# A second weight block loaded ahead of the query weights, and the last stage's order laid anew

## The chip, the cores and the metric

The kernel runs on one core of one Trainium2 chip. The metric is device time in microseconds (us) of one launch, smaller is better. A core has a tensor engine (PE) for matrix products, a vector engine (DVE, VectorE), a scalar engine (ACT, ScalarE), a third general engine (POOL, GpSimd) and a queue engine (SP) that issues DMA transfers. Each engine works through its own instructions in a fixed order and waits by semaphore for the others. PE writes its sums to eight banks of a small memory (PSUM), and ACT or DVE must read a bank out before it can be used again.

## The reference, cut to what matters

One layer of a hybrid decoder on a prompt of 1024 tokens and on 8 x 8 sample tokens that attend to a paged cache of 8192 positions each:

```
n = rmsnorm(h);  u = n @ w_in                       # one projection, split by columns
o_gla = gated linear attention(gq, gk, gv, gg, ga)  # 4 heads
cq = rmsnorm(mq);  q = cq @ mla_w_qup               # 8 heads
k, v = rmsnorm(mkv) @ mla_w_kvup ...
o_mla = attention(q, k, v)                          # causal, and over the cache
h = h + concat(o_gla, o_mla) @ w_o
h = h + conv_ffn(rmsnorm(h))                        # gate, up, conv of width 3, down
h = h + (p @ ple_w_proj) * sigmoid(rmsnorm(h) @ ple_w_gate)
```

The outputs are h for prompt and samples, and the new latents, states and convolution rows. All inputs are float32. Products are made from a high and a low half of each operand (`x = high + low`), as three products: high x high, high x low, low x high. So each weight that is loaded is cast on ACT to its high half and subtracted on DVE or POOL to give its low half before PE can use it.

## The kernel before

The work runs in stages: an opening (sample tokens, the first half of the prompt), a long middle in which the projections, gated linear attention and prompt attention are woven with a stream over the cache blocks, the output projection, the feed-forward part, its last products (by a scheme of seven products instead of eight, the last of them called product 4), and a last stage: the per-layer embedding with its gate.

In the opening and the middle the builder of the program lays each engine's order: it goes by the order of the program as priority and by the readiness that it expects. The opening runs in `prompt_half(0)`. `load_mix(c0)` loads a block of 128 columns of `w_in` (two transfers of 256 KB through the staging buffers `stage`, of which there are three), casts it on ACT and subtracts on POOL, into one of three weight buffers (`wtile`). `load_q` loads the query weights (four transfers of 192 KB, two weight buffers), `load_kv` the key-value weights (two transfers of 256 KB, into two buffers `xin` that the sample work uses too). `mix` runs over blocks: `load_mix`, then `proj` (24 products on PE into `ps_pj`), then `post`, which adds the sample tokens' 8 products (`ps_sm`). The plan is `PLAN = ([0], [], [1, 2, 3])`: block 0 first, none in the second place, then blocks 1, 2, 3, each ahead of the heads of one 128-token tile. The sample tokens' query goes through `sample_q`, `q_finish` (a chain of small DVE and ACT operations; `nwt` is one of them, lines 121 to 125), the transposes `pt_q` (line 439), `ps_qp` (line 443) and `pt_qr` (line 449), under a raised priority.

```
wq = load_q()
wkh, wkl = load_kv()
for i in range(4):
    cT = latents_T(i)
    yield from mix(PLAN[2][i:i + 1])
    yield from heads(i, *cT)
```

In the last stage the order is written out by hand: `LAST` is a string of 370 names of steps, each of which issues an instruction or a few, and every engine keeps the order in which its steps stand in the string. A name's letters are the step, its last digit the tile of 128 rows (t) or the weight chunk (k). Those that the text speaks of:

- `f0`..`f3`: the folds of product 4's four sums into h (DVE, line 2331); `sq` the squares for the norm (ACT, line 1485), `st` a store of the folded part (POOL), `rt` the root (POOL)
- `Y`, `Tb`, `Ta`: four small transposes each of a part of h (PE, line 2202) into one of three banks `pd`; `ry` (line 2553), `ra` copy a turned part out (ACT), `e`, `i`, `g`, `j` form sums of parts (DVE)
- `ac`/`al`, `ic`/`il` and so on: cast (ACT) and low half (DVE) of an operand; `wc`/`wl`, `cc`/`cl`, `zc`/`zl`, `vc`/`vl`, `nc`/`nl`, `xc`/`xl` the same for the weight chunks of the gate's seven products (W, T3, T1, T2, T4, "22"), `c`, `z`, `v`, `n` their sums (DVE)
- `P1t`, `P2t`, `P7t`, `P6t`, `P5t`, `P4t`, `P3t`: twelve products of one tile (PE, `ps_pg`); `P33` is made in two halves. `Jnt`: six products of the embedding (`ps_pj`). `sA`, `sB`, `sC`, `sJ0`, `sJ1`: products of the sample tokens
- `Cq`, `Cv`, `Cw`, `Cx` (gate sum, DVE), `Cs` (sigmoid, ACT), `Cm`, `Ca` (times the embedding, plus h, DVE), `Co` (store of the output); `sd1`, `sk1`, `sm1`, `sa1`: the end of the samples' second half (ACT, DVE, DVE, DVE with a store through POOL); `cv`/`cvc` the convolution's rows; capital `W C Z V X N JL` the loads on SP

Of the kernel before, what the change touches and what calls it, by code (L numbers as in the profile page):

```python
# [18 lines left out]
P = 128  # L19
# [19 lines left out]
LAST = (  # L39
# [14 lines left out]
VIAP = 20  # L54
GS0 = 1
NWB = 10
# [11 lines left out]
def step_kernel(ctx: ExitStack, tc: tile.TileContext, A):  # L68
# [191 lines left out]
    def wtile():  # L260
        return wp.tile([P, 2 * D], F32R, tag="w", name="w")

    def wpair(kc, n):

        w = wtile()
        return tuple(w[:, s * kc * n:(s + 1) * kc * n].rearrange("p (k c) -> p k c", c=n) for s in range(2))

    def load_q():
        return [wload(wp, A["mla_w_qup"][0][:, f * 384:(f + 1) * 384], 2, 384, "w", sbufs=3, out=wpair(2, 384))
                for f in range(2)]  # L270

    def load_kv():
        hl = [wk.tile([P, 1, D], F32R, tag="xin", name="wkv") for _ in range(2)]
        return [w[:, 0] for w in wload(wp, A["mla_w_kvup"][0], 1, D, "w", sbufs=3, out=hl)]

    def load_mix(c0, lo_eng=pool):

        w = wtile().rearrange("p (k s c) -> p k s c", k=8, s=2)
        hl = wload(wp, w_in[:, c0:c0 + P], 8, P, "w", sbufs=3, lo_eng=lo_eng, out=(w[:, :, 0], w[:, :, 1]))
        return hl + (w,)  # L280
# [255 lines left out]
    turned_c, ahead, loads = [], [0], [0]  # L536
# [204 lines left out]
    def prompt_half(hf):  # L741
# [91 lines left out]

        def gates(G, G0):

            with tc.high_priority():
                for x in [G, ggs] + G0:
                    tc.keep_in_program_order(act.activation(x, x, AF.Silu))
                tc.keep_in_program_order(act.preload_act_table_set("natural_log_exp_and_others"))
            put_gates(G, hs)  # L840
            for x, t in zip(G0, (0, 256)):
                put_gates(x, slice(t, t + 256))

        def put_gates(G, ts):
            sp.dma_start(dgg[:, ts].rearrange("(c p) t -> p c t", p=P), G)

        def post(c, st, w, G=None):
# [10 lines left out]
            elif c == 8:  # L858
                for t in (0, 256):
                    x = wk.tile([P, 4, 256], F32, tag="xin", name="G0")  # L860
                    sp.dma_start(x, dgg[:, t:t + 256].rearrange("(c p) t -> p c t", p=P))
                    G0.append(x)

        G0 = []

        def rank():
            pt = pd([P, 4, P], "pt_ga")
# [15 lines left out]
        def mix(chunks, G=None):  # L883
            prev = None
            for c in chunks + [None] * bool(chunks):
                if c is not None:
                    w = load_mix(c * P)
                    st = proj(w, P, G[:, c - 8] if c >= 8 else None)
                    if c == 11 and hf > 0:
                        gates(G, G0)  # L890
                if prev is not None:
                    post(*prev, G)
                prev = (c, st, w)
                yield (5.3 if hf else 7.2) if c is not None else 0.3
# [36 lines left out]
        def heads(i, cTh, cTl):  # L931
# [31 lines left out]
            yield 1.3  # L963

        yield from mix(PLAN[0])
        rank()
        for i in range(4):
            norm_latents(i)
        yield from mix(PLAN[1])
        wq = load_q()  # L970
        wkh, wkl = load_kv()
        for i in range(4):
# [664 lines left out]
    while live_c or live_d:  # L1637
# [4 lines left out]
        else:  # L1642
            w = next(dn, done)
# [307 lines left out]
    with tc.issue_after(z["phl"].ins):  # L1951
# [4 lines left out]
        for i, r in enumerate(raws45):  # L1956
            f, c = i // 2, 4 + i % 2
# [888 lines left out]
```

## Time and profile before

| | us |
|---|---|
| median of 3 runs | 2199.87 (2199.25 to 2206.59) |
| the profiled execution | 2198.96 |
| its span, first to last instruction | 2197.3 |
| PE busy in it | 2121.5 |
| VectorE busy | 1704.0 |
| ScalarE busy | 1384.2 |
| GpSimd busy | 1229.4 |

The mean granted clock of PE is 0.987 of full speed. Times in rows of the profile are from the start of the span. A row of the order of time has the start, the duration, the engine, the line of the kernel, the operation, what it writes and reads, and in brackets how long the engine idled before it and what ended that. A row of the waits has the waiting engine and line, what it waited for, and the sum, the number of times and the longest wait in us. DMA issues stand under SPq or POOLq. Busy times of PE are those of a pipeline: the records of two products overlap, and their spacing is what counts.

### The profile page before, as it was taken

Reading aid. Unit: us, or ns where it says so; the run is one execution under the profiler, and the core shown is the slowest. Engines: PE = TensorE matmul, PEld = TensorE weight load, DVE = VectorE, ACT = ScalarE, POOL = GpSimd, SP = SyncE. Lnnn points to the kernel's source line nnn. Section 1 sums busy time; section 2 is a strip of 40 time slices with the busy share of each in tenths; the row PEclk is TensorE's granted clock in tenths of the full one; section 3 lists DMA queues with packets and bytes.
Section 4 is the critical chain, followed back from the end, with each engine's and each line's share of the span. In section 5 each row is a group of like instructions: output and inputs, shape, how many; then the busy total and the mean of one; then the engine's idle time right before and its main releaser. Section 6 shows DMA issues by size and latency. Waiting matters only on the chain. (4 is left out here: it accounts for less than half of the span.)

```text
span 2197.3 us, 37407 instructions
## 1 busy us (share of the span) xinstructions
PE 2121.5 (97%) x12928; PEld 1901.9 (87%) x12928; DVE 1704.0 (78%) x2611; ACT 1384.2 (63%) x3735; POOL 1229.4 (56%) x1348
## 2 busy tenths in 40 slices
PE   7999999999999999999999999999999999999998
PEld 6888978878888888887898978999999999888787
DVE  4775667377778888887788888788888886887795
ACT  5676766777778888887777776443333334434761
POOL 6675668576677777767454656556566562011211
PEclk9999999999999999999999999999999999999999
DMA  5343245422342222221431223232322325778642
GB/s 184 109 142 111 72 124 159 131 70 61 104 125 65 61 68 66 62 62 42 164 91 61 68 74 118 90 110 82 98 91 93 100 92 193 221 219 245 195 145 84
DMA packets 203576, 244.55 MB, mean 111 GB/s; under 512 B 42940, under 2 KB 137260, under 8 KB 203388
## 3 DMA queue, kind: packets, MB, share of 16 engines
q1 hardware_dynamic: 184428, 181.39, 26.3%
q0 software_dynamic: 17728, 56.31, 8.7%
q10 hardware_dynamic: 1232, 4.46, 0.6%
q8 instruction: 104, 1.70, 0.3%
q14 instruction: 84, 0.69, 0.1%
HBM read 196.39 MB, written 45.67 MB: 110 GB/s over the span
## 5 line engine op out<-in xcount | busy, mean ns | idle before, releaser
L583 ACT ACTIVATE csq<-ks 128x256 f32<-128x256 f32 x1040 | 392.8, 401 | 93.7 <-PE ks L164 82.0
L588 DVE TENSOR_REDUCE css<-csq 128x16 f32<-128x1024 f32 (+1 forms) x264 | 315.7, 1196 | 60.4 <-ACT csq L583 59.2
L138 ACT CAST wh<-st 128x512 fp32r<-128x512 f32 x164 | 100.9, 619 | 169.9 <-PE ps_gu L163 157.6
L162 PE MATMUL ks<-mv0h,cTh 128*128 128x320 f32 (+1 forms) x520 | 171.5, 332 | 7.4 <-ACT sn L585 3.7
L162 PE MATMUL ks<-mv1h,cTh 128*128 128x320 f32 (+1 forms) x520 | 170.1, 329 | 7.6 <-ACT sn L585 3.6
L628 POOL TENSOR_TENSOR chl<-craw,chl 128x1024 fp32r<-128x1024 f32 x64 | 141.5, 2211 | 55.4 <-ACT chl L626 54.8
L163 PE MATMUL ks<-mv1l,cTh 128*128 128x320 f32 (+1 forms) x520 | 153.8, 298 | 0.0
L163 PE MATMUL ks<-mv0l,cTh 128*128 128x320 f32 (+1 forms) x520 | 152.7, 295 | 0.0
L164 PE MATMUL ks<-mv0h,cTl 128*128 128x320 f32 (+1 forms) x520 | 148.2, 298 | 0.9 <-DVE cTl L139 0.8
L164 PE MATMUL ks<-mv1h,cTl 128*128 128x320 f32 (+1 forms) x520 | 148.4, 299 | 0.1
L656 POOL TENSOR_TENSOR phl<-sn,phl 128x512 fp32r<-128x512 f32 (+1 forms) x63 | 84.0, 1334 | 83.1 <-ACT phl L653 82.6
L139 DVE TENSOR_TENSOR wl<-st,wh 128x512 fp32r<-128x512 f32 x124 | 108.6, 879 | 25.8 <-ACT wh L138 25.7
L139 POOL TENSOR_TENSOR wl<-st,wh 128x512 fp32r<-128x512 f32 x40 | 62.0, 1550 | 104.9 <-ACT wh L138 100.1
L163 PE MATMUL ps_dn<-o 128*128 128x512 f32 x308 | 120.2, 390 | 0.1
L164 PE MATMUL ps_dn<-o 128*128 128x512 f32 x308 | 120.2, 390 | 0.0
L139 DVE TENSOR_TENSOR cTl<-ctp,cTh 128x512 fp32r<-128x512 f32 (+1 forms) x136 | 90.0, 662 | 37.5 <-ACT cTh L138 36.5
L162 PEld LDWEIGHTS ks<-mv0h,cTh 128*128 128x128 f32 x520 | 98.6, 190 | 21.4 <-ACT sn L585 8.1
L585 ACT COPY sn<-ks 128x64 f32<-128x64 f32 x520 | 116.8, 225 | 0.0
L162 PEld LDWEIGHTS ks<-mv1h,cTh 128*128 128x128 f32 x520 | 99.3, 191 | 19.8 <-ACT sn L585 7.4
L1333 POOL TENSOR_TENSOR pl<-p,ph 128x512 fp32r<-128x512 f32 (+1 forms) x96 | 97.5, 1020 | 32.7 <-DVE ph L1332 22.7
L162 PE MATMUL ps_dn<-o 128*128 128x512 f32 x308 | 115.8, 391 | 0.0
L164 PE MATMUL ps_gu<-xrh,wl 128*128 128x320 f32 x352 | 108.8, 309 | 0.0
(744 smaller groups left out, 7760.9 us busy)
## 6 DMA issues: line engine op xcount, KB each, us to landing
raw<-ds SPq DMA_DIRECT2D x77, 256.0 KB
raw<-ffn_w_down SPq DMA_DIRECT2D x66, 256.0 KB
stage<-w_in SPq DMA_DIRECT2D x48, 256.0 KB
wr<-ffn_w_down SPq DMA_DIRECT2D x44, 256.0 KB
st<-ffn_w_gate SPq DMA_DIRECT2D x42, 256.0 KB
st<-ffn_w_up SPq DMA_DIRECT2D x42, 256.0 KB
ds<-cv SPq DMA_DIRECT2D x19, 512.0 KB
oraw<-doT SPq DMA_DIRECT2D x16, 256.0 KB
```

Source lines behind the costliest of these rows:

```text
L138: cast = act.copy(hi, src)
L139: res = (lo_eng or dve).tensor_tensor(lo, src, hi.bitcast(F32), ALU.subtract)
L162: pe.matmul(ps, ah, bh, start=first, stop=False)
L163: pe.matmul(ps, ah, bl, start=False, stop=False)
L164: return pe.matmul(ps, al, bh, start=False, stop=last)
L583: act.activation(sq[:, f * 256:f * 256 + 256], ks[:, 0:256], AF.Square)
L585: act.copy(o.sn[:, g0 + i, :], ks[:, 256:320])
L588: dve.tensor_reduce(o.ss[:, g0 + i + 1 - n:g0 + i + 1, :].rearrange("p i h -> p (i h)"), sq2[:, :n].rearrange("p i (h n) -> p (i h) n", n= ...
L628: pool.tensor_tensor(ch[:, c0:c1, 128:256], src, ch[:, c0:c1, 0:128].bitcast(F32), ALU.subtract)
L656: (dve if drain == 2 else pool).tensor_tensor(phl[:, :nt, 64:128], sb, phl[:, :nt, 0:64].bitcast(F32), ALU.subtract)
L1333: pool.tensor_tensor(pl[:, c0:], p[:, c0:], ph[:, c0:].bitcast(F32), ALU.subtract)
```

## The change

Two edits. In the opening, block 1's `load_mix` is called ahead of `load_q` and `load_kv` in the first half of the prompt, and `mix` takes the tile from a dictionary `ahead` in place of loading it; its products and what follows them stay where they were in the program. In the last stage the 370 steps of `LAST` stand in another order. No step is added or left out, and the loads on SP keep their order; among the rest nearly every engine's order differs. The new order begins with the weight casts `wc2`, `wc0`, `wc3` and `cs1`, the folds `f0` to `f3` have few steps of DVE between them, PE begins with `Y0 Y1 Tb0 Ta0 P11` in place of `P10 Y0 Tb0 Ta0 P11`, runs products of tiles 1 and 3 before those of 0 and 2 in part, begins P5 ahead of P6, and ends with `P33 P31 J41 J43 J31 sJ1` in place of `J42 J43 P33`; `sC` and `sJ1` are apart now.

```
@@ LAST (before)
-    "W0 W1 wc1 wc0 wl1 wl0 f0 st0 sq0 C0 wc3 rt0 wc2 wl3 wl2 f1 cs0 C1 st1 sq1 c0 cc0 rt1 cl0 C2 cs1 c1 f2 cc1 sq2 "
-    "st2 cl1 rt2 C3 cs2 c2 P10 f3 cc2 cl2 sq3 st3 JL0 cs3 rt3 c3 Y0 Tb0 ry0 Ta0 i0 cc3 P11 e0 ac0 Z0 jc0_ g0 al0 U0 "
...
-    "P73 N1 z3 yc2 vl2 zs3 yl2 zc3 v3 hy2 zl3 cv vc3 sa0 nc0 JL1 vl3 yc3 n2 nc1 P60 cvc n3 nl1 nl0 nc2 yl3 nc3 P61 "
...
-    "P30 sx sc1 sl1 ss1 J40 Cx0 sm1 Cs40 P31 sa1 Cm40 Ca40 Co40 J41 Cx1 Cs41 P32 Cm41 Ca41 Co41 J42 Cx2 Cs42 J43 "
-    "Cm42 Ca42 P33 Co42 Cx3 Cs43 Cm43 Ca43 Co43 ")
@@ LAST (after)
+    "W0 W1 C0 C1 wc2 wc0 wc3 wl2 cs1 wl0 wc1 f0 cs0 wl3 st0 sq0 wl1 f1 rt0 C2 f2 st1 sq1 c1 sq2 rt1 Y0 f3 C3 st2 Y1 "
+    "ry0 c0 Tb0 rt2 sq3 Ta0 e0 P11 st3 cc0 rt3 i0 ra0 cl0 ac0 g0 JL0 ry1 al0 cs3 Y2 j0 ic0 Tb1 Ta1 ry2 c3 P13 U1 i1 "
+    "ra1 e1 ic1 il0 ac1 cc1 il1 cs2 P10 al1 cc3 cl1 jc0_ cl3 Z0 g1 ec1 j1 Tb2 ec0 Ta2 el1 U0 sA ra2 el0 ac2 jl0_ Ta3 "
...
+    "P73 Cm13 yc0 z2 N1 yl0 zs2 Ca12 hy0 zc2 v2 JL1 P72 yc3 z3 nc0 Co12 zl2 zs3 yl3 vc2 v3 hy3 zc3 P71 yc2 vl2 vc3 "
+    "n2 nc1 zl3 nc2 vl3 P53 yc1 n3 nl2 X0 nc3 yl1 yl2 hy1 P50 nl1 X1 nl3 hy2 nl0 Ca13 Ca10 Co13 P60 sl0 ss0 Co10 sm0 "
...
+    "J40 Cm42 Ca42 P33 Cm40 Co42 Ca40 Co40 P31 Cx3 Cs43 J41 Cx1 Cs41 J43 Cm41 Ca41 J31 Cm43 Co41 Ca43 sJ1 Cm31 Co43 "
+    "Ca31 sd1 Co31 sk1 sm1 sa1 ")
@@ prompt_half
-        G0 = []
+        G0, ahead = [], {}
...
-                    w = load_mix(c * P)
+                    w = ahead.pop(c) if c in ahead else load_mix(c * P)
...
         yield from mix(PLAN[1])
+        if hf == 0:
+            ahead[1] = load_mix(P)
         wq = load_q()
         wkh, wkl = load_kv()
```

16 rows, old and new, of the table LAST are left out of this document.

## The prediction, on record before the changed kernel ran

> **What bounds the kernel now.** I read the page first, then the busy time by stretches for both ends that the change touches, then the waits of the tensor engine (PE) there, then the order of time on each queue.
>
> ```profile
> span 2197.3 us, 37407 instructions
> PE 2121.5 (97%) x12928; PEld 1901.9 (87%) x12928; DVE 1704.0 (78%) x2611; ACT 1384.2 (63%) x3735; POOL 1229.4 (56%) x1348
> ```
>
> PE is busy for 97% of the span, so an edit that leaves its products alone can win no more than its idle time and the time in which its clock was granted at half. The stretches say where these lie (columns: length, then busy time and instruction count of PE, weight load, DVE, ACT, POOL, then granted clock, DMA share, GB/s):
>
> ```profile
> core 0: us, PE busy (x) PEld busy (x) DVE busy (x) ACT busy (x) POOL busy (x), PEclk, DMA share, GB/s
> 44.00:57.80 13.80, 10.18 (x58) 8.78 (x57) 9.62 (x22) 11.24 (x38) 12.54 (x14) 0.99 0.66 204
> 57.80:68.10 10.30, 9.37 (x39) 7.62 (x38) 9.90 (x36) 5.21 (x15) 6.32 (x10) 0.51 0.37 102
> ...
> 100.00:1500.00 1400.00, 1350.46 (x8865) 1205.06 (x8864) 1083.22 (x1740) 1026.71 (x3066) 918.59 (x977) 0.99 0.30 91
> ...
> 2068.00:2092.00 24.00, 19.81 (x95) 15.43 (x94) 20.39 (x32) 17.09 (x34) 4.98 (x9) 0.86 0.39 123
> 2092.00:2191.60 99.60, 99.56 (x444) 80.61 (x443) 76.26 (x118) 40.31 (x66) 18.16 (x33) 1.00 0.37 124
> 2191.60:2197.30 5.70, 0.00 (x0) 0.00 (x0) 2.24 (x6) 0.91 (x2) 0.00 (x0) 0.75 0.14 46
> ```
>
> In the opening PE idles 13.80 - 10.18 = 3.6 us and 0.9 us more, and then runs 10.3 us at 0.51 of its clock, which is 10.3 x 0.49 = 5.0 us of work lost: 9.5 us in all. In the last stage it idles 24.00 - 19.81 = 4.2 us, with a dip of the clock, all of it in the first 24 us; from 2092 to 2191.6 it never stops. After its last product 5.7 us remain. The rows of the waits name what PE waited for, in the opening and then in the last stage:
>
> ```profile
> PE pt_q L439 <- DVE qt L351: 3.6, 1, 3.6
> PE ps_qp L443 <- ACT qT_s L440: 0.9, 1, 0.9
> ```
>
> ```profile
> PE pt L2202 <- ACT h L2553: 1.8, 3, 1.3
> PE pt L2202 <- DVE sg L2557: 1.0, 1, 1.0
> PE pt L2202 <- ACT h L2569: 0.8, 1, 0.8
> PE pt L2202 <- DVE h L2331: 0.7, 1, 0.7
> ```
>
> **The opening, part by part.** Nothing is added or removed. The load of weight block 1 moves: two loads of 256 KB on SP go ahead of four of the query weights (mla_w_qup) and two of the key-value weights; two casts on ACT go ahead of four; two subtractions on POOL go ahead of what POOL then does. These are its queues before:
>
> ```profile
> 44.86 3.25 SPq L180 DMA_DIRECT2D stage<-mla_w_qup  x3
> 49.84 3.43 SPq L180 DMA_DIRECT2D stage<-mla_w_kvup  x2
> 55.89 0.38 SPq L180 DMA_DIRECT2D stage<-w_in  x1
> ```
>
> ```profile
> 51.81 0.51 ACT L138 CAST w<-stage 128x384 fp32r<-128x384 f32 x1
> ```
>
> ```profile
> 65.60 0.62 ACT L138 CAST w<-stage 128x512 fp32r<-128x512 f32 x1 [2.45 <-DMA stage<-w_in]
> ```
>
> ```profile
> 52.48 2.49 POOL L628 TENSOR_TENSOR chl<-craw,chl 128x1024 fp32r<-128x1024 f32 x1
> ```
>
> ```profile
> 66.30 1.28 POOL L139 TENSOR_TENSOR w<-stage,w 128x512 fp32r<-128x512 f32 x1 [1.72 <-ACT w L138]
> ```
>
> The three stage buffers explain the lateness: query and key-value weights held them, so block 1 was asked for at 55.89 and ready only at 66.30 + 1.28 = 67.6. In the new order it takes the place of the first query loads: asked for by 45, cast near 46 to 49, ready near 51, before PE has finished block 0 at 53.9 (57.55 less the wait of 3.6). Then PE holds 24 products and 8 small ones, more than the wait, and could use them. What limits this is that PE's order is fixed when the kernel is built, and the transposes of q (pt_q) have high priority there:
>
> ```profile
> 52.83 2.16 DVE L123 TENSOR_TENSOR nwt<-qrs 64x16 f32<-64x16 f32 x1
> ```
>
> ```profile
> 57.55 0.95 PE L439 MATMUL pt_q<-ident,qt 64*64 64x64 f32 x8 [3.62 <-DVE qt L351]
> ```
>
> This tiny operation on 64x16 took 2.16 us, and ended (54.99) as POOL's 2.49 us subtraction did (54.97); the builder's order can hardly have foreseen that, so it put pt_q right behind block 0. It will do so again, with perhaps a microsecond of block 1 ahead. Two query casts of 0.51 us leave the chain to q, as their tile is now the one that block 0 holds; two of block 1 of 0.62 us enter it further ahead. POOL gets 2 x 1.28 us more before its long subtraction, which may move off the 64x16 operation or onto it. I take the wait as 1.5 us instead of 3.6 and the 0.9 us after it as closed (block 1 fills it): 3.0 us won. The cover of that is block 1's readiness near 51; if POOL makes it late by 3 us or more, nothing is won. Bounds: 9.5 us, all that is lost there; on the other side a loss of 2.6 us, block 1's subtractions standing wholly in the way of q. What is late next is the key-value weights, whose tiles wait for q's last transposes (pt_qr); they are not nearer to PE than before. I keep the dip of the clock at its price, since the last stage's clock fell after waits of 1.3 us at most, 4.2 us in sum.
>
> The Trainium skill, TensorE: Matmul & The Clock Gate, "What's actually happening", has the clock fall after an idle window of about 3.4 us. The opening's 3.6 us agrees; the last stage's 1.3 us does not, unless waits in close sequence count, which the page's "A second HAM failure mode" allows. By the first rule a wait of 1.5 us would give back the 5.0 us too, 8.0 in all; that is the first rival below.
>
> What the builder does between 100 and 1500 us is open: it lays the order there by readiness, from the same program, of which one load is moved. PE's idle there is 1400.0 - 1350.5 = 49.5 us. I take no change, and a tenth of it, 5 us, either way.
>
> **The last stage, part by part.** The same 370 steps in another order; SP's own order is the same letter for letter. So PE's work is the same, and only its waits and the tail count.
>
> ```profile
> 2062.76 1.41 DVE L2509 SCALAR_TENSOR_TENSOR wg<-wp,gkT,wg 128x512 fp32r<-128x512 f32 x2
> 2064.89 0.69 DVE L2331 TENSOR_TENSOR h<-h,ps_dn 128x512 f32<-128x512 f32 x1 [0.72 <-PE ps_dn L164]
> ```
>
> ```profile
> 2074.51 0.68 DVE L2331 TENSOR_TENSOR h<-h,ps_dn 128x512 f32<-128x512 f32 x1
> ```
>
> ```profile
> 2065.62 0.63 ACT L1485 ACTIVATE junk<-h 128x512 bf16<-128x512 f32 x1 [2.79 <-DVE h L2331]
> ```
>
> ```profile
> 2076.52 0.56 ACT L2553 COPY h<-pt 128x512 f32<-128x512 f32 x1
> ```
>
> ```profile
> 2067.64 0.40 PE L164 MATMUL ps_dn<-o 128*128 128x512 f32 x1
> ```
>
> ```profile
> 2185.96 0.23 PE ps_pj L162
> ```
>
> Before: the first fold of product 4 (f0) is at 2064.89, the last (f3) at 2074.51, as weight work stands between them; ACT's first copy of a turned tile (ry0) comes at 2076.52, and PE's transposes stand behind it, as their three banks are held. After: f0 to f3 stand close, so f2 follows its sums, 2 x 1.4 us (six products of 0.23 us in the chain of waits, row 2185.96) behind f0: 67.6, done 68.3. The last product of the stage ahead starts on PE at 2067.64 and ends near 68.0; Y0, Y1, Tb0 (four small transposes each, some 0.4 us) go into the banks that f0, f1, f2 freed. Ta0 needs a fourth: ry0, behind a square of 0.82 us (0.63 and its read of 0.19) that needs f2, then 0.56: 69.7. PE is there at 69.1: 0.6 us of wait, 0.7 with the signal. Then P11 gives 2.8 us (12 products), and in that time VectorE and ACT have e0, i0, ra0, ac0, al0, ry1 done, at some 0.6 us each, all that Y2, Tb1, Ta1 need; then come two products in a row (P13, P10) and the gap cannot reopen there. So 4.2 us of idle become 0.7.
>
> ```profile
> 2081.94 0.63 PE L163 MATMUL ps_pg<-wg,xg 128*128 128x512 f32 x1
> ```
>
> ```profile
> 2085.28 0.40 PE L162 MATMUL ps_pg<-wg,xg 128*128 128x512 f32 x1
> ```
>
> ```profile
> 2124.91 0.60 PE L2772 MATMUL pt_co<-ident,cout 128*44 128x128 f32 x4
> ```
>
> ```profile
> 2125.73 0.68 DVE L2507 TENSOR_TENSOR wg<-wp,wg 128x512 fp32r<-128x512 f32 x1
> ```
>
> With the waits the dip goes: nine products of 0.63 instead of 0.40 (0.2 us apart more, 1.8) and one group of transposes (0.5): 2.3 us. Together 4.2 + 2.3 = 6.5 less 0.7.
>
> What is late next is VectorE. Before, it lowers the last chunk of T2's weights (its 87th step of the stage, vl3) by 2126.4, 63.7 us after its first at 2062.76; PE comes to P60 at 2125.3 and uses that chunk 2.1 us later: 1 us of cover. After, the PE steps ahead of P53 are exactly those ahead of the 2124.91 row, so P53 starts at 2124.9 - 6.5 + 0.7 = 2119.1 and uses the last chunk of T1 (zl3) at 2121.2. That is VectorE's 81st step: at the pace of before 81/87 x 63.7 = 59.3 us, 2122.0; with no waits some 81 x 0.62 (rows of 0.68 that overlap a little) = 50 us, 2113. So 0 to 0.8 us of new wait; I take 0.4. vl3 is its 82nd step and is used 6 us later: covered.
>
> ```profile
> 2170.01 1.10 PE L2746 MATMUL ps_pj<-wj,pts 128*128 128x512 f32 x4
> ```
>
> ```profile
> 2171.81 0.68 DVE L2762 TENSOR_TENSOR fe<-fe,ps_pj 64x512 f32<-64x512 f32 x1
> ```
>
> ```profile
> y_p<-sg POOLq DMA_DIRECT2D x15, 256.0 KB, 2.3
> ```
>
> The tail: PE now ends with the sample's product (sJ1), not P33. Behind it by the rows: 0.7 us to the VectorE addition (2171.81 - 2171.11), three VectorE steps of 0.7, some 0.3 to POOL's store, 2.3 to land: 5.4 us against 5.7, 0.3 won. Sum of this end: 6.5 - 0.7 - 0.4 + 0.3 = 5.7 us won; bounds 6.8 (no new wait) and 2 (the first gap half reopened, 2 us, and VectorE 2 us late).
>
> **Sum.** 3.0 + 5.7 = 8.7 us. The profiled execution took 2198.96 (span 2197.3 and 1.7 around it), 0.9 under the median 2199.87; 2198.96 - 8.7 = 2190.3, on the median's level 2191.
>
> **The rivals.**
> First, the opening recovers in full: PE takes block 1 while it waits, the wait drops so far that the clock holds. For it: 32 products are ready by 51; against it: pt_q stands right behind block 0. Price: 8 to 9.5 us instead of 3.0, so 2185.
>
> Second, the opening doesn't do what it says: PE's fixed order still keeps block 1 behind q, and only the 0.9 closes or not even that. For it: the row of 3.62. Time: 2198.96 - 5.7, with 0.9 for the level, 2194; with a late VectorE in the last stage 2196.
>
> Third, slower: the builder's order between 100 and 1500, with cache blocks and dense work woven by readiness, comes out worse. Place: waits of PE there, 49.5 us now. It decides from 49.5 + 8.7 = 58 us on; at 63 us, a quarter more, 2204. Against it: the order of the program and its weave are the same, only one load moved, and ready work is plenty.
>
> **How the numbers follow.** Chances: the forecast 0.47 (own range 2187 to 2195), first rival 0.23, second 0.22, third 0.08. The bound of 0.5%, 11 us, is about what a measurement of this kernel can tell from no change: faster than 2188.9 needs the first rival (0.20 of its 0.23) or a tail of the forecast (0.07): 0.27. Slower than 2210.9 needs the third rival in a strong form: 0.04. The rest, 0.69, is no change by that bound, though most of it is some microseconds faster. Range 2184 to 2200: from the first rival to an opening that loses its 2.6 us with a last stage that wins 2.
>
> **What would show it.** Opening: both casts of block 1 before 50 us; the wait of pt_q on L351 near 1.5 us (near 0 and a clock of 1.00 between 58 and 68: first rival; 3.6: second). Last stage: idle of PE in its first 24 us down from 4.2 to under 1 us, clock 1.00, folds L2331 within 4 to 5 us of each other, a wait at P53 under 1 us, sJ1 (L2746) last on PE and 5.4 us behind it. Between 100 and 1500: idle 45 to 55 us. The forecast is wrong if that idle moves by 8 us or more, or if a bank or a late chunk stops PE in the middle of the last stage.

## The result, and the profile after

The changed kernel took 2219.78 us (median of 5 runs, 2215.99 to 2221.59) against 2199.87 of the kernel before (5 runs, 2197.34 to 2207.18): a ratio of 1.0091, 95% interval 1.0072 to 1.011. That is 20 us slower, where the forecast was 8.7 us faster. The profiled execution took 2220.88. Its page begins:

```profile
span 2219.1 us, 37463 instructions
...
PE 2125.7 (96%) x12928; PEld 1903.5 (86%) x12928; DVE 1696.5 (76%) x2611; ACT 1385.5 (62%) x3735; POOL 1229.1 (55%) x1348
```

PE is busy 4.2 us longer than before; the other 17.6 of the 21.8 us of longer span are waits and a longer end. The stretches answer to those of before, with the same columns; the last stage's are moved by the 14.3 us that this execution was late there, and the last one begins where PE's work ends:

```profile
44.00:57.80 13.80, 9.29 (x50) 7.86 (x48) 8.89 (x18) 11.46 (x38) 12.82 (x15) 0.94 0.68 210
57.80:68.10 10.30, 9.86 (x47) 8.26 (x47) 8.89 (x29) 4.88 (x14) 6.97 (x14) 0.50 0.47 130
100.00:1500.00 1400.00, 1340.67 (x8779) 1193.51 (x8778) 1065.89 (x1726) 1024.11 (x3057) 906.83 (x969) 0.99 0.30 91
2082.30:2106.30 24.00, 23.38 (x126) 19.20 (x124) 21.99 (x36) 19.35 (x39) 4.70 (x9) 1.00 0.36 121
2106.30:2207.90 101.60, 95.86 (x412) 76.17 (x411) 71.02 (x114) 35.27 (x60) 17.06 (x31) 0.97 0.37 122
2207.90:2219.10 11.20, 0.33 (x2) 0.00 (x0) 2.86 (x5) 0.58 (x1) 1.08 (x2) 0.74 0.20 66
```

Four things are to be read there. The opening idles 4.5 us instead of 3.6. Between 100 and 1500 us PE idles 59.3 us instead of 49.5. The last stage's first 24 us are nearly full (0.6 us idle, clock 1.00), as forecast. But behind them 5.7 us of new idle stand where before stood 0.04, and from the end of the last product (2208.2) to that of the span it is 10.9 us instead of 5.7.

**The opening.** These are PE's one wait, the orders of ACT and POOL, and VectorE's chain to q:

```profile
PE pt_q L439 <- DVE qt L351: 5.0, 1, 5.0
```

```profile
45.79 0.62 ACT L138 CAST w<-stage 128x512 fp32r<-128x512 f32 x1
...
47.87 0.62 ACT L138 CAST w<-stage 128x512 fp32r<-128x512 f32 x1
```

```profile
49.58 1.31 POOL L139 TENSOR_TENSOR w<-stage,w 128x512 fp32r<-128x512 f32 x1
...
51.88 1.29 POOL L139 TENSOR_TENSOR w<-stage,w 128x512 fp32r<-128x512 f32 x1
...
54.26 2.16 POOL L628 TENSOR_TENSOR chl<-craw,chl 128x1024 fp32r<-128x1024 f32 x1
```

```profile
51.81 1.78 DVE L139 TENSOR_TENSOR w<-stage,w 128x384 fp32r<-128x384 f32 x1 [2.98 <-ACT w L138]
53.51 0.35 DVE L123 TENSOR_TENSOR nwt<-qrs 64x16 f32<-64x16 f32 x1
...
54.30 2.66 DVE L350 TENSOR_TENSOR qt<-qt,qrs 64x512 f32<-64x512 f32 x1
```

Before, the 64x16 operation (L123) was the long one, 2.16 us at 52.83, and VectorE's step on q was short:

```profile
55.79 0.68 DVE L350 TENSOR_TENSOR qt<-qt,qrs 64x512 f32<-64x512 f32 x1
```

Both casts of block 1 are done by 48.5. But its second subtraction ran beside VectorE's low half of a query weight, which took 1.78 us (0.56 for the same shape at 52.36 before) and stands in front of the chain to q; and the long subtraction chl moved from 52.48 to 54.26, beside VectorE's step on q: 2.66 us, where it was 0.68. The two are 1.2 and 2.0 us longer, the 64x16 operation 1.8 us shorter (0.35 for 2.16): 1.4 us in sum, as much as the wait grew. So pt_q, still right behind block 0, waited 5.0 us.

**The last stage.** PE's waits there, and the last store:

```profile
PE ps_pj L162 <- ACT wj L2687: 2.0, 1, 2.0
PE ps_pj L162 <- DVE sg L2616: 1.8, 1, 1.8
PE ps_pj L163 <- DVE wj L2691: 1.1, 1, 1.1
PE ps_pj L162 <- DVE h L2581: 0.6, 1, 0.6
```

```profile
2211.33 0.54 POOL L2757 DMA_DIRECT2D y_s<-fd  x1 [1.75 <-DVE fd L2756]
```

```profile
2214.00:2219.10 5.10, 0.00 (x0) 0.00 (x0) 0.00 (x0) 0.00 (x0) 0.00 (x0) 0.50 0.00 0
```

The second fence has the last store in the order of time, the third a stretch in which no engine and no transfer works (DMA share 0.00), though the program has not ended. What lasts is one instruction of POOL's queue, a DRAIN at the end of the program. These are the rows of that line, after and then before (shortest, median and longest in ns, then the first and the last start in us; the longest is the first):

```profile
L2834 POOLq DRAIN  x3: 46/102/7010, 2211.3 to 2218.8; - x3
```

```profile
L2832 POOLq DRAIN  x3: 46/102/7010, 2189.2 to 2197.0; - x3
```

It starts with POOL's last issue, in the changed kernel at 2211.3, and takes 7.0 us. The kernel before has it too, from 2189.2 to 2196.2, but there SP's stores ended at about the same time.

### The profile page after: what moved, and what is told of

It is laid out like the page before. It is cut to its first block, busy times and chain, and to the rows that moved or that the text cites. A ratio compares the mean times of both kernels' runs of the same rounds, so it can differ in the third digit from the quotient of the medians.

```text
span 2219.1 us, 37463 instructions
## 1 busy us (share of the span) xinstructions
PE 2125.7 (96%) x12928; PEld 1903.5 (86%) x12928; DVE 1696.5 (76%) x2611; ACT 1385.5 (62%) x3735; POOL 1229.1 (55%) x1348
## 4 chain that ended last, share of the span: by engine, by line
PE 73%; DVE 8%; issue 7%; ACT 5%; POOL 3%; DMA 3%; SPq 0%; POOLq 0%; DVEq 0%; ACTq 0%
PE ps_gu L164 7%; PE ps_gu L163 7%; PE ps_gu L162 7%; PE ks L162 5%; PE ks L164 4%; PE ks L163 4%; PE ps_dn L163 3%; PE ps_dn L164 3%; PE ps_dn L162 3%; PE cpv L671 2%; PE ctp L545 2%; PE ps_lt L301 2%; DVE css L588 2%; PE ps_pj L162 1%; PE ps_pj L163 1%
## 5 line engine op out<-in xcount | busy, mean ns | idle before, releaser
L615 POOL TENSOR_TENSOR sn<-sn,cy 128x512 f32<-128x512 f32 (+1 forms) x64 | 71.3, 1114 | 74.1 <-DVE cy L613 61.8
```

What stands on the lines that cost most here:

```text
L615: pool.tensor_tensor(snv, snv, y[:, :nt].rearrange("p i h -> p (i h)").unsqueeze(2).broadcast_to([P, nt * 8, 8]), ALU.mult)
```

## Where the time went

Orders differ, so times of named steps say little. Below, PE's products are therefore counted as work: each by the usual distance to the next one for its form (the lower quartile in the trace before), summed in the order of each trace. The column "before" has the time in us at which so much work was done; the others say how much later (+) or earlier it was in one profiled execution of each kernel. The kernels are those of the experiments below. Two executions of one program differ by 3 to 6 us in such a curve ("after" and open_only are one program up to work 1800 and come there at +15.0 and +8.7; nb_a's opening is that of before and shows +4.6), so the curve tells where time goes, and the medians below tell how much.

```
work   before  after open_only open_a open_b open_a2 open_hold   nb_a   nb_b   nb_e last_only last_fix   best
  50     67.0   +1.1    +1.0    +1.4   +0.9   +0.7     -0.1      +4.6   -0.0   +1.8   +1.3     +0.5    +1.8
 100    122.7   -0.2    -0.3    -0.0   -0.5   -0.6     +0.7      +4.6   -0.1   +1.8   +1.3     +0.5    +1.8
 150    176.1   +6.6    +6.5    +6.8   +6.4   +6.1    +12.8      +4.6   -0.1   +1.8   +1.3     +0.5    +1.7
 250    289.6   +0.3    +0.2    +4.0   +0.2   +1.5    +13.5      +4.9   -0.1   +2.7   +2.3     +0.6    +1.6
 350    404.2   +7.1    +6.5    -0.6   +7.3   +1.7    +12.7      +4.9   -0.1   +1.5   +2.3     -0.6    +1.7
 500    592.3  +11.5    +7.8    +0.0  +10.7   +9.3    +16.5     +10.4   +0.2   +2.7   +1.9     +0.5    +1.2
 700    831.1   +9.1    +5.2    -1.6   +8.1  +15.6    +16.7      +8.5   -0.9   +2.9   +1.9     -0.5    +1.1
 900   1073.8  +18.1   +11.7    +1.5  +10.2  +13.5    +14.9     +11.2   -3.0   +1.3   -1.0     -2.3    -4.8
1200   1405.4  +15.0    +8.7    +3.5   +4.4  +15.1    +13.4     +14.8   -8.0   +1.9   -2.5     -3.8    -9.6
1800   2010.1  +15.0    +8.7    +3.5   +4.4  +16.7    +13.4     +15.0   -8.0   +1.9   -2.5     -3.8    -9.6
1900   2118.9   +9.9    +9.0    +2.9   +4.9  +16.2    +13.9     +14.5   -7.3   +2.3   -8.0     -8.9   -14.6
1963   2182.7  +17.3    +9.0    +2.9   +4.9  +16.2    +13.9     +14.5   -7.3   +2.3   -0.4     -7.9   -13.6
```

In "after", the opening costs 1 us, the middle swings between 0 and +18 and leaves 14, the feed-forward part nothing, the last stage wins 5.1 (15.0 to 9.9), loses it and 2.3 more (9.9 to 17.3), and the end adds 10.9 - 5.7 = 5.2.

## The experiments

Theory: the new order of the middle, which the builder lays anew because something ahead of it changed, costs most of the time; the last stage loses by steps that stand behind others in a queue, and by its end. Rivals: the early block itself costs (a weight tile, a staging buffer, GpSimd's time), and the late arrival of loads or engines without room in the last stage.

### Each edit alone

open_only has the change in `prompt_half` and the old `LAST`; last_only has the new `LAST` and the old opening.

> Only the opening's edit, with the last stage's old order. Theory 1 (the 14 us lost ahead of the last stage come from the opening's edit, through the order of the middle that is laid anew): about 2214 us, +14 against before, tensor engine's idle between 100 and 1340 us near 59 us, tail 5.7 us as before. Rival (the two edits act on each other, or the loss ahead of the last stage is chance of single runs): 2197 to 2200 us, with the 3.0 us won that the prediction gave to the opening.

> Only the last stage's new order, with the old opening. Theory 1: everything up to 2060 us as before, the first gap of the last stage closed (6 us won), a wait of some 3 us with a dip of the clock before the fourth product with the second projection's weights, and a tail of some 11.7 us: together about 2207 us, +7. Rival (the last stage's loss is due to other arrival times behind a middle that ran 14 us longer): 2194 us, as predicted for this part.

open_only: 2209.78 us against 2196.72 of before, 1.0061 (1.0044 to 1.0079). last_only: 2205.87, 1.0040 (1.0026 to 1.0054). That is +13.1 and +9.2, together 22.2, against some 20 of both: two separate losses, and no meeting of the two that such runs could tell. Of open_only the profile says

```profile
100.00:1500.00 1400.00, 1342.32 (x8819) 1195.18 (x8818) 1077.47 (x1731) 1025.69 (x3062) 913.20 (x975) 0.99 0.30 91
```

57.7 us of idle in the middle, 8.2 more than before. Of last_only, its first 24 us, the rest up to the last product, and three waits of that rest:

```profile
2068.00:2092.00 24.00, 23.62 (x119) 19.25 (x118) 20.70 (x34) 18.26 (x33) 2.04 (x4) 1.00 0.28 104
2092.00:2189.90 97.90, 92.72 (x397) 73.50 (x396) 68.92 (x111) 33.34 (x57) 17.04 (x31) 0.97 0.38 125
```

```profile
PE ps_pj L162 <- ACT wj L2685: 2.0, 1, 2.0
PE ps_pj L162 <- DVE sg L2614: 1.2, 1, 1.2
PE ps_pj L163 <- DVE wj L2689: 1.1, 1, 1.1
```

The last stage's loss is its own: the same waits come with the old middle ahead of it.

### What made the second projection's weights late

In the new `LAST` the casts `xc0` to `xc3` write the buffers from which the product P62 still reads, and P62 comes later on PE. Behind `xc0` ACT stands still until P62, and `jc1_` behind it:

```profile
2135.99 0.73 ACT L2502 ACTIVATE wg<-wp,gkT 128x512 fp32r<-128x512 f32 x1 [9.56 <-PE ps_pg L164]
...
2138.98 1.03 ACT L2685 CAST wj<-wp 128x1024 fp32r<-128x1024 f32 x1
```

last_wj moves the two conversions:

```
- P51 xc0 w0 Cs20 u3 jc3 q3 xc1 w3 xc2 xl1 P61 jc1_ xl2 Cv3 xc3 jl1_ Cs23 J33
+ P51 jc1_ xc0 w0 Cs20 u3 jc3 q3 xc1 w3 xc2 jl1_ xl1 P61 xl2 Cv3 xc3 Cs23 J33
```

> As the last stage's new order alone, but the two conversions of the second projection's weights (jc1_ on ACT, jl1_ on VectorE) stand ahead of the four gate-weight casts xc0 and xl1 behind which they stood. Theory 1 (they were late only because ACT and VectorE stood at xc0, which has to wait for a tensor product that comes later): the waits of 2.0 and 1.1 us at that product go, and with them the clock's dip of some 2.7 us: 5 us less than the new order alone, about 2202. Rival (the projection's weights came late by DMA, or the queues are full): the wait stays or shows up at the next products, less than 1.5 us won.

2203.08 us against 2196.72, 1.0036 (1.0021 to 1.0050): not told apart from last_only. The wait moved on, as the rival had it, though not for want of room:

```profile
PE ps_pj L162 <- DVE h L2579: 5.0, 1, 5.0
```

```profile
2137.35 1.41 DVE L2509 SCALAR_TENSOR_TENSOR wg<-wp,gkT,wg 128x512 fp32r<-128x512 f32 x2 [4.86 <-ACT wg L2502]
...
2142.59 0.68 DVE L2579 TENSOR_TENSOR h<-h,ps_pg 128x512 f32<-128x512 f32 x1
```

VectorE idles 4.86 us at `xl`, which waits for `xc`, which waits for P62; and `u1` (line 2579), which frees the bank for J20, stands behind it. The stall has two ways round: whatever does not need P62 has to stand ahead of the casts, on both engines.

### What the end consists of

last_sp gives the last store to SP:

```
-            pool.dma_start(A["y_s"][:, f * 512:f * 512 + 512], x)
+            (sp if f else pool).dma_start(A["y_s"][:, f * 512:f * 512 + 512], x)
```

> As the last stage's new order alone, but the sample's last store (y_s, second half) is issued by SP in place of POOL. Theory A (the end of the program waits some 7.2 us from POOL's last issue, whatever lands): POOL's last issue is now the store ahead of it, 2.3 us earlier, so the span ends 2.3 us earlier. Theory B (only the last transfer counts, and POOL's is slow to be reported): by SP it ends as before's tail did, 3.5 us behind the issue: 4 to 4.5 us earlier. Theory C (the tail is long for another reason): no change within 0.5 us.

2202.65 us against 2196.72, 1.0020 (1.0009 to 1.0031). The span ends at 2198.5; POOL's and SP's last issues are

```profile
2190.83 0.54 POOL L2624 DMA_DIRECT2D y_p<-sg  x1 [2.17 <-DVE sg L2619]
```

```profile
2192.85 0.50 SPq L2755 DMA_DIRECT2D y_s<-fd  x1
```

From the end of POOL's last issue to the end of the span: 2198.5 - 2191.37 = 7.1 us, though SP's store came 2 us later. In the changed kernel it is 2219.1 - 2211.87 = 7.2, in last_only 2201.7 - 2194.42 = 7.3. From the last product, which took its place 0.8 us earlier here, the end came 2.4 us sooner; theory A said 2.3. last_wj, with POOL's store last, has 2200.1 - 2192.89 = 7.2. So the program does not end before some 7.2 us behind POOL's last issue, whatever lands: that is POOL's DRAIN of 7.0 us and the few closing steps behind it. The DRAIN stands at the end of all 17 traces, right at POOL's last issue, with 6.8 to 7.0 us. What POOL does in it no record shows. In the kernel before POOL's last issue ended at 2189.73, and 7.2 later is 2196.9: just under the 2197.3 that SP's stores gave.

### The last stage repaired

last_fix, on the old opening (a line "..." leaves steps out):

```
- J10 Cq2 zc0 v1 zc1 Cs12 J12 zl0 vc1 Cm10
+ J10 Cq2 Cm10 zc0 v1 zc1 Cs12 J12 zl0 vc1
...
- P51 xc0 w0 Cs20 u3 jc3 q3 xc1 w3 xc2 xl1 P61 jc1_ xl2 Cv3 xc3 jl1_ Cs23 J33 jc1 xl3 jl1 P62 jl3 ha1 xl0 u1 ha3
-  q1 J23 jc2 u2 jl2 J20
+ P51 jc1_ w0 Cs20 u3 jc3 q3 w3 jl1_ P61 Cv3 Cs23 J33 jc1 u1 q1 jl1 jl3 ha1 ha3 P62 xc0 xc1 xc2 xc3 J23 u2
+  xl0 xl1 xl2 xl3 jc2 jl2 J20
...
- Co40 P31 Cx3 Cs43 J41 Cx1 Cs41 J43 Cm41 Ca41 J31 Cm43 Co41 Ca43 sJ1 Cm31 Co43 Ca31 sd1 Co31 sk1 sm1 sa1
+ Co40 sJ1 Cx3 sd1 Cs43 sk1 sm1 sa1 P31 J41 Cx1 Cs41 J43 Cm41 Ca41 J31 Cm43 Co41 Ca43 Cm31 Co43 Ca31 Co31
...
-   (sp if tail else pool).dma_start(A["y_p"]...
+   (sp if tail or (n, t) in ((4, 1), (3, 1)) else pool).dma_start(A["y_p"]...
-   pool.dma_start(A["y_s"]...
+   (sp if f else pool).dma_start(A["y_s"]...
```

> The last stage's new order on the old opening, with three repairs: what does not need the product P62 stands ahead of the casts that do, on ACT and VectorE both (jc1_, jl1_, u1, q1, jl1, jl3 ahead of xc0 to xl3); one VectorE step (Cm10) stands earlier; the sample's product and its steps stand ahead of P31, and the last stores are issued by SP. Theory 1 (the new order lost by steps queued behind casts that had to wait, and by POOL's end): the waits of 2.0, 1.1, 0.6 and 1.2 us and the dip go, some 7 us, and the tail falls from 12 to about 5.5 us: 2205.9 - 13.5, about 2192, 4 us under before. Rival (VectorE or ACT have no room in this order, so the wait moves on as it did when the weights alone were moved): 2198 or more.

2192.36 us against 2197.99, 0.9974 (0.9964 to 0.9984): 5.6 us faster than before, 14.8 under last_only by the differences to before. The span is 2187.6. The rest up to the last product, and the two waits over 0.3 us that are left:

```profile
2100.00:2182.90 82.90, 80.96 (x358) 64.29 (x356) 62.77 (x100) 29.57 (x51) 15.91 (x29) 1.00 0.37 126
```

```profile
PE ps_pg L162 <- DVE sg L2614: 1.2, 1, 1.2
PE ps_pj L162 <- DVE sg L2614: 0.4, 1, 0.4
```

```profile
2181.85 3.04 SPq L2624 DMA_DIRECT2D y_p<-sg  x4
```

Idle in that rest is 1.9 us, with the clock at 1.00, and the end comes 2187.6 - 2184.89 = 2.7 us behind SP's last issue, as before (2197.3 - 2194.61 = 2.7). With that the last stage's first gain is kept: in the table of work, last_fix wins 5.1 us up to work 1900 and gives 1.0 of it back.

### The opening's own wait

open_hold is open_only with the first long subtraction of the cache blocks held until VectorE has scaled q:

```
-        eng.tensor_tensor(qn, qn, gqk[:rows]...
+        z["qn"] = eng.tensor_tensor(qn, qn, gqk[:rows]...
...
-   with tc.issue_after(twice.ins) if o.n > NB * 8 - 3 else nullcontext():
+   with tc.issue_after(twice.ins if o.n else z["qn"].ins) if o.n > NB * 8 - 3 or not o.n else nullcontext():
```

> The opening's edit alone, and the subtraction for the first cache block on GpSimd (chl, 128x1024) is held until VectorE has scaled q; old order of the last stage. In the opening: theory 1 (VectorE's step on q took 2.66 us for 0.68 because GpSimd's long subtraction ran beside it) says that the step takes 0.7 us and the wait of pt_q falls from 5.0 to 2.5 to 3.2 us. Rival (q is late by its weights' casts): the wait stays at 4.5 to 5. For the middle the order comes out anew again: by the theory of chance order between -5 and +15 us against before.

```profile
PE pt_q L439 <- DVE qt L351: 3.0, 1, 3.0
```

```profile
55.54 0.68 DVE L350 TENSOR_TENSOR qt<-qt,qrs 64x512 f32<-64x512 f32 x1
```

```profile
57.80:68.10 10.30, 9.99 (x40) 8.04 (x38) 8.98 (x38) 5.73 (x21) 6.28 (x13) 0.52 0.47 128
```

Theory 1: VectorE's step is back at 0.68 us, and the wait fell by the 2 us. So it was GpSimd's long subtraction beside it that stretched it. The Trainium skill, SBUF — State Buffer, "Who interferes with whom", has VectorE operations with two inputs in SBUF contend with GpSimd operations that read it, the later one standing still until the other is done; the rows of 2.66 and 0.68 us agree. The clock was still granted at 0.52 behind a wait of 3.0 us, so a smaller wait than the 3.6 of before brings the dip too.

The clock records of the 17 traces tell what it goes by. Every fall to half begins on a grid of steps of 3.41 us, and the share of the step just ahead in which PE was busy, by the busy times of the profile, goes with it: of 98 steps at full clock with PE busy for less than half, 93 were followed by half the clock; of 372 between 0.5 and 0.8, 49; of 10100 above 0.8, two. Such a step and the half clock behind it, here and then in the last stage of the kernel before, where no wait was longer than 1.3 us:

```profile
54.75:58.16 3.41, 0.60 (x8) 0.47 (x8) 3.31 (x11) 1.48 (x5) 3.08 (x5) 1.00 0.64 173
58.16:68.40 10.24, 9.98 (x35) 8.09 (x36) 8.83 (x38) 5.37 (x20) 6.00 (x12) 0.50 0.45 124
```

```profile
2074.93:2078.34 3.41, 1.59 (x9) 0.84 (x7) 2.64 (x5) 3.06 (x7) 1.46 (x3) 1.00 0.93 313
2078.34:2085.17 6.83, 5.66 (x17) 4.52 (x18) 6.65 (x11) 5.71 (x11) 0.00 (x0) 0.50 0.15 55
```

So in these traces it is the idle time summed over one such step that goes with a dip, not the length of a single wait.

As a whole it took 2209.93 us against 2197.99, 1.0054 (1.0038 to 1.0071). Its order of the middle is another one again, and shows in one place what such an order can do. GpSimd's operations and VectorE's stretched one, and what waited for it:

```profile
133.80 3.72 POOL L139 TENSOR_TENSOR w<-stage,w 128x512 fp32r<-128x512 f32 x3
137.47 1.07 POOL L615 TENSOR_TENSOR sn<-sn,cy 128x512 f32<-128x512 f32 x1
```

```profile
133.18 5.52 DVE L199 TENSOR_TENSOR rqb<-qt,ropep 128x128 f32<-128x128 f32 x1
```

```profile
140.13 0.38 ACT L583 ACTIVATE csq<-ks 128x256 f32<-128x256 f32 x1 [6.66 <-DVE css L588]
```

```profile
140.67 0.58 PE L162 MATMUL ks<-mv0h,cTh 128*128 128x256 f32 x1 [6.37 <-ACT sn L585]
```

An operation of VectorE on 128x128 (0.28 us for its neighbour at line 200) lasted until a run of four operations of GpSimd was done; ACT stood 6.66 us for a step of VectorE's behind it (css), and PE 6.37 us for ACT. That is read from rows, not tried. Nor does the sum of such stretches tell the orders apart: VectorE's time over the lower fifth of each operation and shape between 70 and 1370 us is 83 to 96 us in all of these traces, 94 in before and 90 in the changed kernel. That what counts is whether PE waits behind one is argued, not tried.

### The middle: the early block, or the order?

Of these kernels, open_mid has the early load between the query and the key-value weights; nb_a, nb_b and nb_e are the kernel before with one number changed by which the builder weaves cache blocks and dense work, and which no engine sees; open_a and open_b have the early block and the same numbers, open_a2 a third order (`GS0 = 2` beside the 10.0).

```
nb_a, open_a:  -  yield 10.3 if hf else 12.2      +  yield 10.3 if hf else 10.0      (first value product)
nb_b, open_b:  -  yield 10.3 if hf else 12.2      +  yield 10.3 if hf else 14.0
nb_e:          -  yield (5.3 if hf else 7.2)      +  yield (5.0 if hf else 7.2)
open_a2:       open_a and  -  GS0 = 1             +  GS0 = 2
open_mid:      -  ahead[1] = load_mix(P), then load_q(), load_kv()     +  load_q(), ahead[1] = load_mix(P), load_kv()
```

> The opening's edit alone, but block 1's load stands between the query weights and the key-value weights, not ahead of both; old order of the last stage. Theory 1 (the loss is that of the order between 100 and 1340 us, which comes out anew with any change ahead of it and has no tie to where the load stands): the loss there can be anything between -5 and +15 us against before, and its stalls stand at other places than with the load ahead of both. Rival (the early block itself costs, by a weight tile and a stage buffer held longer): a loss like that of the opening's edit alone, 10 to 15 us, with stalls at the same places.

> The kernel before with one number changed that no engine sees: the weave of cache blocks and dense work takes the first value product as 10.0 us in place of 12.2. The first 1285 rows of the tensor engine's order stay as before, the rest is laid anew. Theory 1 (a new order in the middle moves the time by some 5 to 15 us by itself, nothing of the opening needed): a difference of over 4 us to before, all of it between 200 and 1340 us. Rival (the middle takes such changes without loss; it is the early block that costs): within 3 us of before.

> The kernel before with that cost as 14.0 us in place of 12.2: the first 2973 rows of the tensor engine's order stay, up to about 490 us. Theory 1 (a new order costs, and the order of before is a good one among many): 3 to 12 us slower, all behind 490 us. Rival (only orders changed ahead of 490 us cost): within 3 us of before.

> The kernel before with the weave's cost of a second-half mix block as 5.0 us in place of 5.3: the first 4345 rows of the tensor engine's order stay, up to about 690 us. Theory 1: a smaller share of the order is new, so a smaller loss, 0 to 8 us, all behind 690 us. Rival (only orders changed early cost): within 3 us of before.

> The opening's edit alone with the weave's cost of the first value product as 10.0 us (the change that alone cost the kernel before 13 us); old order of the last stage. Theory 1 (each new order of the middle draws its own waits, with no tie to the opening): not the sum of the two losses, 26 us, but something of its own between +5 and +17 us against before. Rival (the two losses have causes of their own and add): about +26 us.

> The opening's edit alone with the same cost as 14.0 us; the tensor engine's first 3035 rows stay those of the opening's edit, up to about 500 us. Theory 1: the lag of the opening's edit at 500 us is kept, and from there on it differs: between +2 and +17 us at the end against before. Rival (the loss belongs to the opening's edit): +13 us, within 2.

> The opening's edit with the cost of 10.0 us and the sample's part of the linear attention woven in one step later (GS0 = 2), old order of the last stage; the tensor engine's first 2217 rows stay those of the run with 10.0 alone, whose lag at 350 us was -0.6 us. Theory 1 (order alone): anything from -3 to +13 us against before, all of it behind 370 us. Rival (the early block has a price of its own of some 5 us): +5 us or more, as with every order that held the early block so far.

| kernel | early block | median, us | before beside it | ratio, 95% interval |
|---|---|---|---|---|
| open_only | yes | 2209.78 | 2196.72 | 1.0061 (1.0044 to 1.0079) |
| open_mid | yes, later | 2211.10 | 2197.99 | 1.0061 (1.0044 to 1.0077) |
| open_hold | yes | 2209.93 | 2197.99 | 1.0054 (1.0038 to 1.0071) |
| open_a | yes | 2202.95 | 2197.59 | 1.0024 (1.0014 to 1.0034) |
| open_b | yes | 2203.41 | 2197.59 | 1.0025 (1.0013 to 1.0036) |
| open_a2 | yes | 2214.19 | 2198.40 | 1.0069 (1.0054 to 1.0083) |
| nb_a | no | 2211.24 | 2197.99 | 1.0063 (1.0040 to 1.0085) |
| nb_b | no | 2194.67 | 2197.59 | 0.9988 (0.9978 to 0.9997) |
| nb_e | no | 2201.77 | 2197.59 | 1.0021 (1.0011 to 1.0031) |

nb_a settles that a new order alone can cost this much: one number of the weave, the first 1285 rows of PE's order kept, and the kernel before loses 13 us without an early block; nb_b wins 2.9 by the same number turned the other way. The stretch between 100 and 1500 us of nb_a, then of nb_b, shows 58.6 and 47.0 us of idle, beside 49.5 of before and 59.3 of the changed kernel:

```profile
100.00:1500.00 1400.00, 1341.37 (x8804) 1193.89 (x8803) 1075.38 (x1730) 1025.68 (x3065) 903.89 (x971) 0.99 0.30 91
```

```profile
100.00:1500.00 1400.00, 1353.03 (x8911) 1207.08 (x8910) 1080.27 (x1749) 1029.57 (x3070) 916.08 (x979) 0.99 0.30 92
```

The losses do not add: the early block (+13.1) and the 10.0 (+13.3) give +5.4 together. Nor do they stand at fixed places behind work 250: the table of work has open_only 6.5 us late at 350, open_a not, and open_hold late by nothing more from 500 on. Ahead of that there is one place in common: between work 100 and 150 all six kernels with the early block fall back by 6 us or more (open_mid, which the table leaves out, by 6.4), in three different orders (open_only, open_a, open_b and open_a2 share theirs up to there), and none of the others does. At least three of the six have made that good by work 250. Of nb_b the expectation was wrong in its sign (a loss of 3 to 12 us): orders better than that of before exist. nb_e lost 4.2 us, all of it in later parts, within its band; of open_b's +5.8 the rival (13, within 2) is out. Two runs fit the rival as well or better: open_mid lost what open_only did, with stalls at the same places (its curve is +9.3 at work 150, +3.0 at 250, +8.3 at 350, beside +6.5, +0.2, +6.5), so a later place of the load changed little; and open_a2's +15.8 lies over the theory's band. What stays open: the six orders with the early block all lost 5 us or more, the four without it (with before) came out from -2.9 to +13.3. PE's idle between 100 and 1500 us is 56.7 to 60.8 us in all six, 47.0 to 58.6 in the four. That leans towards a price of some 5 us of the early block, but draws so few, and partly alike, do not tell it from chance. Against such a price speaks that open_a, with the early block, was not late at work 700; full_fix, the same program up to the last stage, was 2.3 us late there.

### Both ends repaired, and a version that beats both

full_fix is the whole change with the 10.0 of open_a, the repairs of last_fix and one more (`J12 zl0 vc1 Z2 n0 sJ0 Cm12 J13` becomes `J12 zl0 Cm12 vc1 Z2 n0 sJ0 J13`). best has the same last stage, the old opening and the 14.0 of nb_b.

> The whole change, with the weave's cost of 10.0 us and the last stage repaired as before, and one VectorE step more (Cm12) ahead of a weight step in place of behind it. Theory 1 (order, last stage's waits and the tail are separate terms that add): +5.3 of the opening's edit with that cost, -5.6 of the repaired last stage, -1 of the added repair: 1 us under before, 20 us under the whole change. Rival (they act on each other): over 4 us away from that.

> Without the early block: the weave's cost of 14.0 us, and the last stage repaired in the same way. By adding: -2.8 and -5.6 and -1, together 9.4 us under before, near 2188. Rival (the gain of 14.0 was chance or is lost with another end): 2192 or more.

full_fix: 2199.90 us against 2198.40, 1.0005 (0.9996 to 1.0014): 1.5 us over before, 2.8 from the sum, so the terms add as far as such runs can tell. best: 2186.84 against 2198.40, 0.9947 (0.9934 to 0.9960), 11.6 us faster than the kernel before, and by the differences to before some 31 faster than the changed one.

```profile
span 2182.1 us, 37400 instructions
```

```profile
100.00:1500.00 1400.00, 1353.15 (x8932) 1208.54 (x8931) 1081.32 (x1753) 1031.54 (x3076) 917.37 (x982) 0.99 0.30 92
```

The middle has nb_b's idle again, 46.9 us.

## Why the prediction was wrong, step by step

From 8.7 us faster to 20 slower is a miss of some 29 us. By the table and the runs it is made up of about 4 in the opening, 13 in the middle, 7 by the new waits of the last stage, 1 in its first gap and 5.5 in the tail; these agree with 29 within the scatter of the curve.

- **Opening, loads and casts.** Right: both casts before 50 us, and pt_q right behind block 0, as said. Block 1 was ready at 53.2 (51.88 + 1.29) where 51 was taken, which cost nothing by itself, since PE's order did not use it.
- **Opening, the wait of pt_q: 1.5 us taken, 5.0 measured.** The step that failed is "with perhaps a microsecond of block 1 ahead" together with GpSimd's 2 x 1.28 us "which may move off the 64x16 operation or onto it". None of block 1 came ahead of pt_q, and the long subtraction moved off the 64x16 operation onto a later step of the same chain. The prediction had both halves in hand, as the second rival's place and as the bound "block 1's subtractions standing wholly in the way of q", and chose the middle. The price of the opening as a whole was small: 1 us late at work 50, where 3.0 us were to be won.
- **Opening, the dip.** It stayed, as taken: 0.50 of the clock behind 5.0 us, and 0.52 behind the 3.0 of open_hold. That is partly luck, since it was taken for a wait of 1.5 us. The reason given, that waits of 1.3 us at most had brought a dip in the last stage, fits the count of steps. The Trainium skill, TensorE: Matmul & The Clock Gate, "What's actually happening", has about 3.4 us of idle for it; the 3.0 is under that, and the measurement decides. No run has a wait of 1.5 us there. Estimated from the count of steps: if all of it fell into one step, PE would be busy for 0.56 of it, and 28 of the 87 steps between 0.5 and 0.6 were followed by a dip.
- **Middle, no change, 5 us either way: +13 us measured (open_only).** This is the step that decided the case. "The order of the program and its weave are the same, only one load moved" is no ground for the same time, since the builder lays out all that follows anew. nb_a shows that this alone can cost 13 us; whether some 5 of the 13 belong to the early block itself stays open. The third rival named place and mechanism, and its threshold of idle was met (59.3 us, where it decided from 58), as was the prediction's own sign of being wrong (idle moved by 8 us or more: 9.8); but it had 0.08, where of the nine new orders above eight lost 4 us or more, and five of them over 10. Its price was low too: 58.6 us of idle in nb_a went with 13 us, where the rival had 63 us for a slower result of 2204.
- **Last stage, the first gap.** Right: 4.2 us of idle became 0.6, the clock 1.00, and 5.1 to 5.5 us were won by the table of work, where 5.8 were forecast.
- **Last stage, the new wait.** The wrong place. At P53 nothing shows; VectorE was late at J13 (1.8 us), and the main stall, 3.7 us and a dip of the clock, stood at J23 and J20. The prediction counted how many steps VectorE had done by a due time and looked at no queue for a step that had to wait for a later product. Its last sign, "a late chunk stops PE in the middle of the last stage", is what happened.
- **The tail: 5.4 us taken, 10.9 measured.** The chain up to the store was right: 3.1 us (2208.2 to 2211.3), as 0.7 + 2.1 + 0.3. The failed term is "2.3 to land": the end came 7.2 us behind POOL's last issue, and the prediction carried over a landing time from the middle of the stage to the program's last transfer on that queue. POOL's DRAIN of 7.0 us stands in the trace of before as well; moving POOL's last issue to the end put it in the open.

## What to carry to other kernels

When the builder lays an order by expected readiness, any edit ahead draws a new order for all that follows; here eight of nine new orders lost, perhaps because the order that is there had been picked among many. Try a few draws (a weave number that no engine sees) on both sides before a few microseconds are put down to the edit, and compare traces by work done, not by named steps. In an order written by hand, ask of each step what it waits for and which product frees that; whatever stands behind it on the same engine waits too, and moving a single victim only hands the wait to the next. And look at what each queue does at the program's end: here POOL's last issue had to lie some 5 us ahead of SP's (7.2 against 2.7 us to the end) to cost nothing.

## What the hardware showed that was not expected

- The program ended 7.1 to 7.3 us behind the end of POOL's last DMA issue (four kernels in which that end came last, last_sp among them), a DRAIN on POOL of 7.0 us, with the transfer done long before: in the changed kernel nothing moved from 2214 to 2219.1. Behind SP's last issue it was 2.7 us (before and last_fix).
- A 128x128 operation of VectorE took 5.52 us beside four operations of GpSimd in a row, not the length of one of them.
- The clock fell to half at steps of a grid of 3.41 us, and of 98 steps with PE busy for less than half, 93 were followed by it. A wait of 3.0 us did it (open_hold), and so did several of 1.3 us at most (the kernel before, 1.59 us busy of 3.41).
